# Second layer of a two-layer backbone: query latent and gates as seven products of quarters

## The chip, the cores and the metric

The kernel runs on one core of a Trainium2 chip. Its engines work side by side, each through its own list of instructions in order: TensorE (PE; its weight loads are listed apart as PEld), VectorE (DVE), ScalarE (ACT), GpSimd (POOL), and SyncE (SP), whose queue here issues nearly all DMAs; a few go through ScalarE's. TensorE writes to eight PSUM banks of 512 float32 per partition; everything else lies in SBUF (128 partitions) or in device memory. The metric is the device time of one execution in microseconds, the median over runs.

## The reference, cut to what matters

Two layers over 1024 latent tokens and 256 context tokens, width 1024. Layer 0 is windowed attention, layer 1 is multi-head latent attention, which is the last layer, so that context tokens need only keys and values there. For layer 1, with h the normed and modulated input:

```
cq, ckv, kr, g = split(h @ w_in, [512, 768, 800])      # 512 + 256 + 32 + 1024 columns
q  = rms_norm(cq, q_norm) @ w_uq                       # 16 heads x (64 + 32)
kv = rms_norm(ckv, kv_norm) @ w_ukv                    # 16 heads x (64 + 64)
qr, kr = rope(q[..., 64:]), rope(kr)
p  = softmax((qn . kn + qr . kr) * 96 ** -0.5)
y  = ((p @ v) * silu(g)) @ w_out
```

For the 1024 latent tokens, cq and g together are one product: 1536 channels, inner length 1024, 1024 tokens.

## The kernel before, in words

Every float32 operand of the large products is cut in two: a high half, rounded to the matmul's fp32r type by ScalarE, and a low half, the difference, mostly by VectorE or GpSimd (`split`, L272 and L273). `mm3` (L277 to L279) then makes three matmuls: high x high, low x high, high x low. So a product with 128 channels, inner length 1024 and 512 tokens is 8 x 3 = 24 matmuls of 512 columns.

Two large SBUF arenas, R (fp32r halves) and F (float32), are laid out by hand: `r_at` and `f_at` take an offset in KB per partition. PSUM banks are taken in turn (`pss`, `pst`).

The order of the instructions from late in layer 0's projections to the end of layer 1's projections isn't that of the program. A planner (`Plan`) records each operation with the operations that it must wait for (found by overlapping rectangles of memory, `rect`), and `emit` then lays them out by a simulation: each engine takes, of what is ready, the operation that comes first in the program; TensorE may reach 40 operations ahead. Durations and delays come from `Plan.cost` (for VectorE on 512 columns from SBUF 0.03 + 512 x 0.00106 us). What it lays out is each engine's fixed order; semaphores hold it to the dependencies at run time. After `plan.emit(tensor=5.0)` (L1834) the rest is issued in program order.

Layer 1 before the change goes through these stages:

- kv (L1437 to L1482): ten tiles of 128 tokens. Layer 0's result is loaded from `x1_d`, normed, turned by TensorE (`turn1`, L1368), scaled and shifted (`h1_part`), and cut into `hT1`: five buffers of 256 tokens, with input channels on the partitions. `kv_mm` makes 24 matmuls of 288 columns a tile. The latent's weights are loaded and cut meanwhile (`wq_cut`).
- query latent (`cq_tile`, L1262): eight tiles of 128 tokens, tokens on the partitions, 24 matmuls of 512 columns each (the first and last tile: 48 of 256). The squared sum of the row (L1206), its root, and a scaling by row and by `qn` follow; then four transposes (L1281) and a cut give `cqT` with channels on the partitions.
- queries (`qr_tile`, `qn_tile`): eight rotary tiles and sixteen others, 12 matmuls of 512 each; results are cut and stored to `qr_d` and `qn_d`. The rotary ones take a multiplication (L1300) and a shuffle (L1301) on VectorE and two operations on GpSimd (L1302, L1303).
- gates (`g_tile`, L1335): four blocks of 256 channels, each 2 x 2 tiles of 128 channels and 512 tokens, 24 matmuls, Silu on ScalarE (L1350), a store to `g1_d`. The last two blocks' tiles for the second token half (`gs`, L1835) aren't in the plan: they stand, in program order, between the first attention unit's top scores.
- attention, sixteen units of a head pair and 512 queries: `top` (L1623) makes high-half scores whose maxima VectorE reduces (L1629), `turn` (L1637) and `shift` (L1641) bring the maxima to the queries' side, `score` (L1657) makes the scores, ScalarE the exponentials, `PV` (L1680) the values' sum. A unit's top scores are made during the unit before it; the first unit has none before it.

```python
    gs = [g_tile(bi, 1, c, PB[:, 6 + c, :]) for bi in (8, 9) for c in range(2)]
    next(gs[0])
    for b in range(4):
        for i in range(3):
            units[0].top([(b, i)], (PB[:, 2 * i, :], PB[:, 2 * i + 1, :]))
        if b:
            next(gs[b])
        next(gs[b])
```

`make_V` (five pieces of 12 matmuls of 256 columns), `make_K` and `make_kr` prepare values and keys of the first heads.

Of the kernel before, what the change touches and what calls it, by code (L numbers as in the profile page):

```python
# [21 lines left out]
SEQ = 1024  # L22
# [45 lines left out]
class Plan:  # L68
# [9 lines left out]
    @staticmethod  # L78
    def rect(ap):
        t, dims = ap.tensor.name, [tuple(d) for d in ap.ap]  # L80
        row = int(np.prod(ap.tensor.shape[1:]))
        if t.split("_")[-1] == "d" or "_d_" in t or dims[0][0] != row:
            return t, 0, 1, ap.offset, ap.offset + sum(s * (n - 1) for s, n in dims) + 1
        p, f = divmod(ap.offset, row)
        return t, p, p + dims[0][1], f, f + sum(s * (n - 1) for s, n in dims[1:]) + 1
# [22 lines left out]
    def add(self, eng, name, fn, a, k, line):  # L108
# [7 lines left out]
        for w, xs in ((False, aps), (True, writes)):  # L116
            for x in xs:
                t, p0, p1, f0, f1 = self.rect(x)
# [91 lines left out]
def kernel(ctx: ExitStack, tc: tile.TileContext, t, out, dbg=None):  # L210
# [967 lines left out]
    wst1 = [96, 48, 96, 96, 48, 96, 48, 96, 48, 96]  # L1178
    ckvT = r_at(114, 2, 2, TOK)
    cqT = [r_at(64, 4, SEQ), r_at(134, 4, SEQ)]  # L1180
    cosb = f_at(0, 8, 32)
    sinb = f_at(1, 8, 32)
    qn = f_at(8, 512)
    kvn = f_at(66, 256)
    stg = Ring(F, [30, 32, 64.25], 512)
# [4 lines left out]
    ukV = r_at(64, 2, 2, 1024)  # L1190
# [3 lines left out]
    blocks1 = [("kv", 512, 288), ("cq", 0, 256), ("cq", 256, 256)]  # L1194
    blocks1 += [("qr", 1024, 512), ("qn", 0, 512), ("qn", 512, 512)]
    blocks1 += [("g", 800 + c * 256, 256) for c in range(4)]
    wt1 = {}

    def fetch1(bi, eng=None):
        kind, c0, n = blocks1[bi]  # L1200
        nk = 4 if kind[0] == "q" else 8
        wt1[bi] = r_at(wst1[bi], 2, nk, n)
        load_w(wt1[bi], t["b_w_uq"] if kind[0] == "q" else w_in1, stg, nk, n, lo_eng=eng, col0=c0)
# [15 lines left out]
    def kv_mm(ti):  # L1219
        p, j = ti // 2, ti % 2  # L1220
        W = wt1[0]
        kvps[ti] = ps = pss()
        for k in range(8):
            mm3(
                ps[:, 0:288],
                [hT1[p][:, s, k, j * 128 : j * 128 + 128] for s in range(2)],
                [W[:, s, k, :] for s in range(2)],
                k == 0, k == 7,
            )
# [29 lines left out]
    wcq = R[:, 48 * KB : 144 * KB].rearrange("p (c n) -> p c n", c=2)[:, :, 0 : 16 * KB]  # L1259
    wcq = wcq.rearrange("p c (s k n) -> p c s k n", s=2, k=8)  # L1260

    def cq_tile(ti):  # L1262
        p, j = (ti + 2) // 2, ti % 2
        ps = pss()
        for c in {0: (0, 1), 7: (1, 0)}.get(ti, (slice(0, 2),)):
            o = ps[:, c * 256 : c * 256 + 256] if ti in (0, 7) else shp(ps, 2, 256)
            for k in range(8):
                mm3(
                    o,
                    [hT1[p][:, s, k, j * 128 : j * 128 + 128] for s in range(2)],  # L1270
                    [wcq[:, c, s, k, :] for s in range(2)],
                    k == 0, k == 7,
                )
        r = rstd(ps, 512, sm_ring())
        e = ev.next()
        nc.vector.scalar_tensor_tensor(e, ps, r, qn, ALU.mult, ALU.mult)

        def rest():
            pt = shp(pst(), 4, 128)
            for c in range(4):  # L1280
                nc.tensor.transpose(pt[:, c, :], e[:, c * 128 : c * 128 + 128], ident)  # L1281
            ts = slice(ti * 128, ti * 128 + 128)
            split(cqT[0][:, :, ts], cqT[1][:, :, ts], pt)

        pend.append(rest)
# [3 lines left out]
    def qr_tile(c, half):  # L1289

        W = wt1[3]
        ts = slice(half * 512, half * 512 + 512)
        ps = pss()
        for k in range(4):
            mm3(
                ps, [W[:, s, k, c * 128 : c * 128 + 128] for s in range(2)], [cqT[s][:, k, ts] for s in range(2)],
                k == 0, k == 3,
            )
        a, r = ev.next(), ev.next()
        nc.vector.tensor_mul(a, ps, cosq[:, ts])  # L1300
        nc.vector.stream_shuffle(out=r, in_=ps, mask=swap1)  # L1301
        nc.gpsimd.tensor_mul(r, r, sinq[:, ts])  # L1302
        nc.gpsimd.tensor_add(a, a, r)  # L1303

        def rest():
            q = shp(qst.next(), 2, 512)
            split(q[:, 0].bitcast(F32R), q[:, 1].bitcast(F32R), a)
            load(out=qr_d[c, :, :, ts], in_=q)

        pend.append(rest)  # L1310

    def qn_tile(bi, pair, half):
        W = wt1[bi]
        c = pair % 4
        ts = slice(half * 512, half * 512 + 512)
        ps = pss()
        for k in range(4):
            mm3(
                ps, [W[:, s, k, c * 128 : c * 128 + 128] for s in range(2)], [cqT[s][:, k, ts] for s in range(2)],
                k == 0, k == 3,  # L1320
            )
        q = shp(qst.next(), 2, 512)
        split(q[:, 0].bitcast(F32R), q[:, 1].bitcast(F32R), ps)
        load(out=qn_d[pair, :, :, ts], in_=q)


    gpairs = [(2, 3), (4, 1)]
    gview = [
        R[:, o * KB : (o + 2 * d) * KB].rearrange("p (q n) -> p q n", q=2)[:, :, 0 : 16 * KB].rearrange(
            "p q (s k n) -> p q s k n", s=2, k=8  # L1330
        )
        for o, d in ((0, 16), (32, 48))
    ]

    def g_tile(bi, gp, c, ps=None):  # L1335

        c0 = blocks1[bi][1]
        W = wt1[bi]
        ps = pss() if ps is None else ps
        for k in range(8):  # L1340
            mm3(
                shp(ps, 2, 256),
                [W[:, s, k, c * 128 : c * 128 + 128] for s in range(2)],
                [gview[gp][:, :, s, k, :] for s in range(2)],
                k == 0, k == 7,
            )
            if k in (2, 5):
                yield
        gg = ev.next()
        nc.scalar.activation(gg, ps, AF.Silu)  # L1350
        ch = (c0 - 800) // 128 + c
        if gp == 0:
            load(out=g1_d[ch, :, 256:768], in_=gg)
        else:
            load(out=g1_d[ch, :, 768:1024], in_=gg[:, 0:256])
            load(out=g1_d[ch, :, 0:256], in_=gg[:, 256:512])
        yield

    def g_whole(bi, gp, c):
        for _ in g_tile(bi, gp, c):  # L1360
            pass
# [8 lines left out]
    def h1_part(p, b):  # L1370
        w = 1 if p == 0 else 0
        ps, h = tbank.pop((p, b)), shp(hr.next(), 2, 256)
# [3 lines left out]
        nc.vector.tensor_scalar(h[:, 0], ps[:, 0], sa[:, 0], sb[:, 0], ALU.mult, ALU.add)  # L1376

# [8 lines left out]
    wt1[0] = r_at(wst1[0], 2, 8, 288)  # L1386
# [6 lines left out]
    def w0_cut1(k, eng):  # L1393
        split(wt1[0][:, 0, k], wt1[0][:, 1, k], kws[k], eng)
# [50 lines left out]
    wq = {}  # L1445
    wq1 = Ring(F, [22, 24, 26, 28], 512)
    wq2 = Ring(F, [48, 50, 52, 54], 512)

    def wq_cut(c, i, eng):
        ks = slice(2 * i, 2 * i + 2)  # L1450
        split(wcq[:, c, 0, ks, :], wcq[:, c, 1, ks, :], wq[2 + 4 * c][i], eng)

    two = turn_two()
    for ti in range(NT):
# [15 lines left out]
        if ti in (2, 6):  # L1470
            wq[ti] = []
            for i in range(4):
                wq[ti].append(shp((wq1 if ti == 2 else wq2).next(), 2, 256))
                src = w_in1[i * 256 : i * 256 + 256, 64 * ti - 128 : 64 * ti + 128]
# [509 lines left out]
```

## Time and profile before

| what | value |
|---|---|
| median of 3 runs | 1500.04 us (1500.01 to 1501.14) |
| span of the profiled execution | 1499.7 us |
| profiled execution's own time | not listed apart; the runs' median is 0.3 us over the span |
| PE busy | 1479.0 us, 99% |
| DVE, POOL, ACT busy | 960.6, 850.2, 708.7 us |
| granted TensorE clock, mean | 0.997 |
| DMA, mean | 119 GB/s |
| kv stage, about | 682 to 720 us |
| query latent to first score | 720.35 to 940.72 us |

The page gives for each engine its busy time; the chain of waits follows the work that ended last back from the end. Matmuls are pipelined, so that the duration printed of one is longer than the distance between two starts; the distances say what a matmul costs. A row of the view in order of time has start, duration, engine, line, operation, tile written and read, shape, count, and in brackets how long the engine sat idle before and what ended that. A row of the view by groups has busy time and mean ns of one after the bar. A row of the view by stretches has the stretch, its length, and the busy us and instructions of PE, PEld, DVE, ACT and POOL, then granted clock, DMA share and GB/s.

### The profile page before, as it was taken

Reading aid. Unit: us, or ns where it says so; the run is one execution under the profiler, and the core shown is the slowest. Engines: PE = TensorE matmul, PEld = TensorE weight load, DVE = VectorE, ACT = ScalarE, POOL = GpSimd, SP = SyncE. Lnnn points to the kernel's source line nnn. Section 1 sums busy time; section 2 is a strip of 40 time slices with the busy share of each in tenths; the row PEclk is TensorE's granted clock in tenths of the full one; section 3 lists DMA queues with packets and bytes.
Section 4 is the critical chain, followed back from the end, with each engine's and each line's share of the span. In section 5 each row is a group of like instructions: output and inputs, shape, how many; then the busy total and the mean of one; then the engine's idle time right before and its main releaser. Section 6 shows DMA issues by size and latency. Waiting matters only on the chain.

```text
span 1499.7 us, 25035 instructions
## 1 busy us (share of the span) xinstructions
PE 1479.0 (99%) x9164; PEld 1203.9 (80%) x9164; DVE 960.6 (64%) x1869; ACT 708.7 (47%) x1363; POOL 850.2 (57%) x774
## 2 busy tenths in 40 slices
PE   6999999999999999999999999999999999999998
PEld 4888888888888888889888888776777767876687
DVE  4787788648778888878454004575566566566764
ACT  4421222369887888875233421453344434443322
POOL 2563365356454444457246510598788788789371
PEclk9999999999999999999999999999999999999999
DMA  9555644664354232334128622303121222121442
GB/s 338 164 170 170 209 157 166 212 209 117 120 159 126 86 108 89 95 120 135 35 85 287 198 70 85 92 15 79 47 60 54 62 63 60 47 59 34 154 155 85
DMA packets 128339, 178.93 MB, mean 119 GB/s; under 512 B 11980, under 2 KB 80716, under 8 KB 128216
## 3 DMA queue, kind: packets, MB, share of 16 engines
q1 hardware_dynamic: 123816, 170.67, 36.2%
q10 hardware_dynamic: 4400, 6.66, 1.3%
q8 instruction: 72, 1.18, 0.3%
q14 instruction: 51, 0.42, 0.1%
HBM read 131.13 MB, written 46.15 MB: 118 GB/s over the span
## 4 chain that ended last, share of the span: by engine, by line
PE 93%; DMA 2%; issue 2%; DVE 2%; POOL 1%; ACT 1%; SPq 0%; POOLq 0%; ACTq 0%; DVEq 0%
PE PB L277 15%; PE PB L278 15%; PE PB L279 15%; PE PB L1657 13%; PE PB L1680 9%; PE PB L729 5%; PE PB L1623 5%; PE PB L719 5%; PE PB L689 3%; PE PB L690 3%; PE PB L898 1%; PE PB L1691 1%; DMA arena_f<-x 1%; PE PB L748 1%; PE PB L903 1%
## 5 line engine op out<-in xcount | busy, mean ns | idle before, releaser
L277 PE MATMUL PB<-arena_r 128*128 128x512 f32 (+2 forms) x1240 | 452.0, 365 | 0.0
L278 PE MATMUL PB<-arena_r 128*128 128x512 f32 (+2 forms) x1240 | 446.0, 360 | 0.4 <-DVE arena_r L273 0.3
L279 PE MATMUL PB<-arena_r 128*128 128x512 f32 (+2 forms) x1240 | 445.5, 360 | 0.0
L1673 POOL TENSOR_TENSOR arena_f<-arena_f 128x1024 f32<-128x1024 f32 x120 | 285.7, 2381 | 8.2
L277 PEld LDWEIGHTS PB<-arena_r 128*128 128x128 f32 x1240 | 234.0, 189 | 44.4 <-issue 9.2
L279 PEld LDWEIGHTS PB<-arena_r 128*128 128x128 f32 x1240 | 233.9, 189 | 34.3
L278 PEld LDWEIGHTS PB<-arena_r 128*128 128x128 f32 x1240 | 234.1, 189 | 33.2 <-POOL arena_r L273 1.1
L1657 PE MATMUL PB<-arena_r 64*128 64x512 f32 (+1 forms) x1600 | 225.8, 394 | 0.0
L1629 DVE TENSOR_REDUCE krF<-PB 128x1 f32<-128x512 f32 (+1 forms) x264 | 167.3, 678 | 78.7 <-PE PB L1623 78.7
L1667 ACT ACTIVATE arena_f<-PB 128x1024 f32<-128x1024 f32 x160 | 164.2, 1026 | 111.6 <-PE PB L1657 83.6
L273 POOL TENSOR_TENSOR arena_r<-arena_f,arena_r 128x512 fp32r<-128x512 f32 (+1 forms) x98 | 132.6, 1368 | 143.0 <-ACT arena_r L272 128.7
L273 DVE TENSOR_TENSOR arena_r<-PB,arena_r 128x512 fp32r<-128x512 f32 (+2 forms) x215 | 139.9, 662 | 76.3 <-ACT arena_r L272 75.5
L1657 PEld LDWEIGHTS PB<-arena_r 64*128 64x128 f32 (+1 forms) x1600 | 176.5, 185 | 14.3 <-issue 5.2
L696 DVE CUSTOM_DVE_ANT_0 arena_f<-PB,arena_f,small 128x256 f32<-128x256 f32 (+1 forms) x288 | 148.3, 525 | 51.6 <-PE PB L690 33.3
L272 ACT CAST arena_r<-PB 128x512 fp32r<-128x512 f32 (+2 forms) x215 | 119.8, 563 | 110.1 <-PE PB L279 73.4
L1680 PE MATMUL PB<-arena_f 128*64 128x512 f32 x640 | 145.9, 595 | 0.0
L702 ACT ACTIVATE arena_f<-arena_f,small 128x640 f32<-128x640 f32 (+2 forms) x160 | 119.0, 744 | 15.5 <-DVE small L696 13.9
L499 DVE SCALAR_TENSOR_TENSOR arena_f<-arena_f,small 128x512 f32<-128x512 f32 x98 | 113.2, 1199 | 10.5 <-DMA arena_f<-ada_w 10.2
L729 PE MATMUL PB<-arena_r 128*128 128x512 f32 x336 | 118.6, 429 | 0.0
L1623 PE MATMUL PB<-arena_r 64*128 64x512 f32 (+1 forms) x768 | 109.4, 354 | 0.0
L719 PE MATMUL PB<-ident,arena_f 128*128 128x128 f32 x672 | 108.6, 272 | 0.1
L1680 PEld LDWEIGHTS PB<-arena_f 128*64 128x64 f32 x640 | 44.0, 137 | 79.6 <-issue 78.6
(189 smaller groups left out, 1972.6 us busy)
## 6 DMA issues: line engine op xcount, KB each, us to landing
arena_f<-ada_w SPq DMA_DIRECT2D x96, 256.0 KB, 3.9
arena_r<-q_d SPq DMA_DIRECT2D x160, 128.0 KB, 2.9
arena_f<-a_w_in SPq DMA_DIRECT2D x40, 256.0 KB, 3.8
arena_f<-x SPq DMA_DIRECT2D x16, 512.0 KB, 6.1
q_d<-arena_f SPq DMA_DIRECT2D x16, 512.0 KB, 3.0
qn_d<-arena_f SPq DMA_DIRECT2D x16, 512.0 KB, 4.7
arena_r<-qn_d SPq DMA_DIRECT2D x16, 512.0 KB, 5.3
arena_f<-b_w_in SPq DMA_DIRECT2D x24, 256.0 KB, 4.5
```

The lines of the kernel that those rows point to most:

```text
L273: (lo_eng or nc.vector).tensor_sub(lo, src, hi.bitcast(F32))
L277: nc.tensor.matmul(o, ah, bh, start=first, stop=False)
L278: nc.tensor.matmul(o, al, bh, start=False, stop=False)
L279: nc.tensor.matmul(o, ah, bl, start=False, stop=last)
L719: nc.tensor.transpose(pt[:, h, :], self.Ps[h][:, ci * 128 : ci * 128 + 128], ident)
L729: nc.tensor.matmul(self.pv, V[:, self.chunks[ci], self.g, :], PT[:, s], start=ci == 0 and s == 0, stop=ci == self.m - 1 and s == 1,)
L1623: nc.tensor.matmul(bank[:, o : o + n], self.q[r, s, bs], k[r, 0, n0 : n0 + n], start=s == 0, stop=s == 2)
L1629: nc.vector.reduce_max(self.mxp[:, e, b : b + 1, i], bank[:, 0:n], AX.X)
L1657: nc.tensor.matmul(PB[:, b + e, :], k[r, s, cs], q[r, sq], start=i == 0, stop=i == 4)
L1667: nc.scalar.activation(E, PB[:, b : b + 2, :], AF.Exp)
L1673: eng.tensor_add(acc, acc, E)
L1680: nc.tensor.matmul(PB[r, 7, :], Vq[:, c, h, :], E[:, e], start=c == 0, stop=c == NT - 1)
```

## The change

Query latent and gates become one product of weights (as rows: 1536 channels) with activations, in six sets of 256 channels: two of the latent, four of gates. In each set the weights A (256 channels x 1024) and the activations B (1024 x 1024 tokens) are cut into quarters, and Winograd's form of Strassen's scheme gives the four quarters of the result by seven products of quarters, where the plain way has eight. A product is 128 channels, inner length 512, 512 tokens: `product`, 4 x 3 = 12 matmuls.

- The activations' four combinations (`t_make`, T1 to T4) are made once, for all sets, in float32 by VectorE, and cut (`t_cut`). For that, `h1_part` also copies each scaled tile from SBUF to SBUF by DMA into `hF` (sixteen copies of 256 KB on SP's queue). T1 and T4 overwrite quarters of `hT1` that are done with.
- The weights' four combinations (`s_make`) are made per set, on VectorE, a set ahead. Weights come in quarters of 128 channels by 512 rows, 256 KB each (`w_load`), 36 loads, two quarters of a set twice.
- First come the six products A11 B11 (kept in SBUF by ScalarE), then the six A12 B21, whose sum is a result quarter, then per set the other five (`set_steps`), whose sums are put together by VectorE from PSUM. Sets go in the order 0, 2, 1, 3, 4, 5, where 0 and 1 are the latent's.
- The query latent comes out with channels on the partitions, so its 32 transposes fall away. The row scale is now found by summing squares over sets and partitions (`cq_sums`, eight matmuls of one column), spread over the partitions by GpSimd and eight transposes (`cq_spread`), and applied to the queries: in the rotary tables, and by a multiplication of each other query tile. `q_norm` goes into the query weights as they are cut (`q_cut`).
- All queries now come behind the gates. The last eight query tiles are in the plan with `make_kr` and `make_K`; `make_V`, in five pieces, takes the place of the gate tiles between the first unit's top scores.
- The planner's rectangles are finer: an access with up to four widely spaced parts counts as several rectangles, and bf16 offsets are put in words.

The code that the diff adds or moves, cut:

```diff
+    def product(W, B):
         ps = pss()
         for k in range(4):
+            m = [B(s, k) for s in range(2)]
+            mm3(ps if len(m[0].shape) == 2 else shp(ps, 2, 256), [W[s][:, k] for s in range(2)], m, k == 0, k == 3)
+        return ps
...
+    def done(i, c, t, x):
+        if i > 1:
+            nc.scalar.activation(x, x, AF.Silu)
+            tok_store(g1_d[2 * i - 4 + c], x, t)
+            return
+        dst = cqT[2 * i + c, t]
+        split(dst[:, 0], dst[:, 1], x)
+        sq = x if summed[t] else acc[t]
+        nc.scalar.activation(sq, x, AF.Square)
+        if summed[t]:
+            nc.vector.tensor_add(acc[t], acc[t], x)
+        summed[t] += 1
+
+    def t_make(k):
+        f1, f2, f3, f4 = (shp(f[:, k], 2, 256) for f in (F1, F2, F3, F4))
+        nc.vector.tensor_sub(f1, H12(k), H11(k))
+        nc.vector.tensor_sub(f2, H22(k), f1)
+        nc.vector.tensor_sub(f3, H22(k), H12(k))
+        nc.vector.tensor_sub(f4, H21(k), f2)
...
+    def s_make(st):
+        a11, a21, a22, a12, s1 = st
+        nc.vector.tensor_add(s1, a21, a22)
+        nc.vector.tensor_sub(a21, a11, a21)
+        nc.vector.tensor_sub(a11, s1, a11)
+        nc.vector.tensor_sub(a12, a12, a11)
+        for x in (a11, a21, s1, a12, a22):
+            yield w_cut(x)
+
+    def set_steps(i, W):
+        p1 = p1s[i]
+        ps = product(W[0], T2)
+        q = outs.next()
+        nc.vector.tensor_add(q, ps, p1)
+        yield
+        p7 = product(W[1], T3)
+        yield
+        ps = product(W[2], T1)
+        r, x = outs.next(), outs.next()
+        nc.vector.tensor_add(r, ps, q)
+        nc.vector.tensor_add(x, p7, r)
+        nc.vector.tensor_add(q, p7, q)
+        done(i, 1, 1, x)
+        yield
+        ps = product(W[3], B22)
+        nc.vector.tensor_add(r, ps, r)
+        done(i, 0, 1, r)
+        yield
+        ps = product(W[4], T4)
+        nc.vector.tensor_add(q, ps, q)
+        done(i, 1, 0, q)
+        yield
...
+    def qn_tile(bi, c, t):
+        ps = q_mm(bi, c, t)
+        e = ev.next()
+        nc.vector.tensor_mul(e, ps, rbc[t])
+        q_out(qn_d[4 * bi - 4 + c], e, t)
...
+        if p:
+            load(out=hF[p][:, 2 * b : 2 * b + 2, :], in_=h)
...
+    for i, o in enumerate((8, 10, 6, 12, 2, 4)):
+        ps = product(W1[i], B11)
+        p1s[i] = f_at(o, 512)
+        nc.scalar.copy(p1s[i], ps)
+        flush()
+        if i == 0:
+            W1[5] = w_cut(a11[5])
+            a12[5] = w_load(a11r.next(), 5, 0, 1)
+        if i < 4:
+            t_cut(T2, F2, i)
+            t_cut(T1, F1, i)
+        for j in {3: (2, 3), 4: (4, 5), 5: (0, 1)}.get(i, ()):
+            a12r[j] = w_cut(a12[j])
+    W = []
+    ops = iter(())
+    for n, i in enumerate((2, 3, 4, 5, 0, 1)):
+        ps = product(a12r[i], B21)
+        x = outs.next()
+        nc.vector.tensor_add(x, ps, p1s[i])
+        done(i, 0, 0, x)
+        if n == 1:
+            ops = s_make(st.pop())
+            st.append(s_load(1, order[1]))
+        if n:
+            W += [w for _, w in zip(range(1), ops)]
+        if n < 4:
+            t_cut(T3, F3, n)
+            t_cut(T4, F4, n)
...
     plan.emit(tensor=5.0)
-    gs = [g_tile(bi, 1, c, PB[:, 6 + c, :]) for bi in (8, 9) for c in range(2)]
-    next(gs[0])
+    fillb = Banks(6, 7)
+    vk = make_V(0)
+    next(vk)
     for b in range(4):
         for i in range(3):
             units[0].top([(b, i)], (PB[:, 2 * i, :], PB[:, 2 * i + 1, :]))
-        if b:
-            next(gs[b])
-        next(gs[b])
+        next(vk)
```

368 lines of the change are left out of this document (200 added, 168 removed).

## The prediction

> **What bounds the kernel now.** I read the page's busy shares and its chain of waits first, to see which engine sets the end.
>
> ```profile
> span 1499.7 us, 25035 instructions
> PE 1479.0 (99%) x9164; PEld 1203.9 (80%) x9164; DVE 960.6 (64%) x1869; ACT 708.7 (47%) x1363; POOL 850.2 (57%) x774
> PE 93%; DMA 2%; issue 2%; DVE 2%; POOL 1%; ACT 1%; SPq 0%; POOLq 0%; ACTq 0%; DVEq 0%
> ```
>
> TensorE (PE) is busy 99% and carries 93% of the chain, so a matmul removed is worth its pitch, provided the other engines keep up. The average says nothing of the stage that changes, so the second view is the instructions in order of time: it gives the ends of the stage and the pitch of its matmuls.
>
> ```profile
> 720.35 0.36 PE L277 MATMUL PB<-arena_r 128*128 128x256 f32 x1
> ...
> 723.07 0.28 PE L278 MATMUL PB<-arena_r 128*128 128x256 f32 x1
> ...
> 724.51 0.28 PE L278 MATMUL PB<-arena_r 128*128 128x256 f32 x1
> ...
> 728.50 0.39 PE L277 MATMUL PB<-arena_r 128*128 128x512 f32 x1
> ...
> 730.54 0.39 PE L277 MATMUL PB<-arena_r 128*128 128x512 f32 x1
> ...
> 737.62 1.03 PE L1281 MATMUL PB<-ident,arena_f 128*128 128x128 f32 x8
> 738.41 0.48 PE L277 MATMUL PB<-arena_r 128*128 128x512 f32 x1
> ...
> 938.76 0.44 PE L1637 MATMUL PB<-ident,krF 128*64 128x128 f32 x4
> 939.13 0.50 PE L277 MATMUL PB<-arena_r 128*128 128x512 f32 x1
> ...
> 940.72 0.97 PE L1657 MATMUL PB<-arena_r 64*128 64x512 f32 x6
> ```
>
> The printed 0.39 us is a latency; starts give the pitch. From 728.50 to 730.54 there are nine 512-wide matmuls: 0.227 us each. From 723.07 to 724.51 there are twelve of 256: 0.120 us. Eight transposes take 0.79 us (737.62 to 738.41): 0.10 each. The stage begins with the first query-latent matmul at 720.35 and ends with the first score matmul at 940.72: 220.4 us. The third view is busy time by stretch:
>
> ```profile
> core 0: us, PE busy (x) PEld busy (x) DVE busy (x) ACT busy (x) POOL busy (x), PEclk, DMA share, GB/s
> 720.30:940.70 220.40, 220.12 (x1091) 183.37 (x1089) 68.87 (x121) 62.38 (x118) 76.13 (x64) 1.00 0.38 125
> 682.00:727.00 45.00, 44.07 (x347) 43.74 (x346) 37.56 (x94) 23.16 (x62) 31.86 (x40) 1.00 0.28 88
> 660.00:682.00 22.00, 22.00 (x126) 18.95 (x125) 15.90 (x27) 17.00 (x39) 12.28 (x14) 1.00 0.77 252
> ```
>
> PE fills the stretch, VectorE (DVE) uses 68.9 of 220.4 us, and the clock is full. Matmuls bound this stage; DVE has room, and the change spends that room.
>
> **The change, part by part.** *Matmuls.* Before, query latent and gates cost 6 tiles x 24 of 512, 2 tiles x 48 of 256, and 16 gate tiles x 24 of 512: 528 x 0.227 + 96 x 0.120 = 131.4 us. After, six sets of seven products of 12 matmuls, 504 x 0.227 = 114.4 us: **-17.0 us**. The 24 query tiles, the twelve matmuls each, keys and values stay.
>
> *Transposes.* 32 of the latent go; 8 that spread the row scale come: 24 x 0.10 = **-2.4**. Eight one-column matmuls for the sums of squares are new; the nearest row is the four small matmuls L1637, 0.37 us from 938.76 to 939.13, so about 0.09 each: **+0.7**. With nothing hidden worse than before, that is -18.7.
>
> *Work moved to DVE and ScalarE.* I need the price of a DVE operation with both inputs in SBUF, with GpSimd (POOL) idle and not.
>
> ```profile
> L603 DVE TENSOR_TENSOR arena_r<-arena_f,arena_r x8: 684/685/686, 258.4 to 276.1; 64x512 fp32r<-64x512 f32 x8
> L273 DVE TENSOR_TENSOR arena_f<-PB,arena_f 128x512 fp32r<-128x512 f32 x16 | 11.0, 689 | 24.3 <-ACT arena_f L272 24.3
> 783.50 1.11 DVE L273 TENSOR_TENSOR arena_f<-arena_f 128x512 fp32r<-128x512 f32 x1
> L1302 POOL TENSOR_TENSOR arena_f<-arena_f 128x512 f32<-128x512 f32 x8 | 10.4, 1296 | 1.5 <-DVE arena_f L1301 1.5
> L1301 DVE STREAM_SHUFFLE arena_f<-PB 128x512 f32<-128x512 f32 x8 | 6.0, 747 | 0.0
> L499 DVE SCALAR_TENSOR_TENSOR arena_f<-arena_f,small x98: 730/752/1857, 72.8 to 297.4; 128x512 f32<-128x512 f32 x98
> L272 ACT CAST arena_r<-arena_f 128x512 fp32r<-128x512 f32 x44 | 26.3, 623 | 21.6 <-DMA arena_f<-b_w_ukv 7.9 <-DMA arena_f<-b_w_in 6.0 <-DMA arena_f<-b_w_uq 5.0
> 738.45 0.58 ACT L272 CAST arena_r<-PB 128x512 fp32r<-128x512 f32 x1
> 739.06 0.69 DVE L273 TENSOR_TENSOR arena_r<-PB,arena_r 128x512 fp32r<-128x512 f32 x1 [0.32 <-ACT arena_r L272]
> ```
>
> 0.69 us from either memory; 1.11 us where POOL's rotary multiply runs beside it. Counted from the code, DVE has in the product stage: 16 differences of the activations; 62 low halves (16 for the four combinations T, 8 first factors left over, 30 for the combined weights, 8 for the latent); 24 combinations of weights; 42 additions of products; 6 sums of squares. 150 x 0.69 = 103 us beside 114.4 us of matmuls. The cover holds, but 90% full where it was 31%. ScalarE has 62 casts at 0.62, 6 copies at 0.58 and 24 functions at about 0.6, some 56 us: covered. It is tightest at the start: the first six products need only ready factors, but the second six need more cuts, and the third row T2 after twelve products, 12 x 12 x 0.227 = 32.7 us. By then DVE owes some 16 differences, 24 cuts, 6 additions and the first set's 9: 55 x 0.69 = 38 us, of which a third of the differences can run in the idle DVE time of the stage before (45.0 - 37.6 = 7.4 us). 38 - 5 = 33 against 32.7, and an order laid out by the planner at 0.573 us per operation (its cost line), 17% too short. So a stall from 0 to 38 - 32.7 = 5.3 us; nearer the low end, since T1, T3 and T4 are wanted one to four products later: **+2**. Six PSUM banks let PE run five products ahead of the additions after that.
>
> *Stage before: copies of the activations.* Sixteen 256 KB SBUF copies are added on SP's queue; each waits for the scaled tile, and behind it stand layer-input and weight loads. Four of them fall into the crowded stretch (660 to 682, 252 GB/s), where 1 MB takes 4 us; the later ones meet DMA at 28%. The inputs so delayed are due several tiles later, and PE's slack was 0.9 us. Between 0 and 4, nearer the low end for that lead: **+1**.
>
> *Query tiles.* DVE: rotary tiles 8 x (0.69 + 0.75 + 1.11), others 16 x 1.38, twelve scaled cuts at 0.75, eight value and key cuts at 0.69, 57 us under 24 x 12 x 0.227 = 65 us. The first scaled cuts fall into the last set, where no weights are made. No cost; if cover fails, the banks lend 13 us first. Stores become 36 issues on SP instead of 24, at under 0.5 us each, also covered.
>
> *The first unit's maxima.* Here a cover is removed. Four gate tiles stood between the groups of top-score matmuls; five pieces of V stand there now.
>
> ```profile
> 914.00 1.43 PE L1623 MATMUL PB<-arena_r 64*128 64x512 f32 x12
> 919.00 1.43 PE L1623 MATMUL PB<-arena_r 64*128 64x512 f32 x12
> L1629 DVE TENSOR_REDUCE krF<-PB 128x1 f32<-128x512 f32 x20 | 12.5, 684 | 13.3 <-PE PB L1623 13.3
> L1629 DVE TENSOR_REDUCE krF<-PB 128x1 f32<-128x256 f32 x8 | 3.0, 415 | 0.0
> L1634 DVE TENSOR_REDUCE krF<-krF 128x8 f32<-128x24 f32 x1 | 0.2, 178 | 0.0
> 939.25 1.41 DVE L1641 TENSOR_TENSOR arena_r<-PB,ident 4x512 fp32r<-4x512 f32 x2 [2.04 <-PE PB L1637]
> 941.52 0.62 PE L1623 MATMUL PB<-arena_r 64*128 64x512 f32 x4
> ```
>
> Reductions: 16 x 0.684 + 8 x 0.415 = 14.3 us, 3.6 a group; PE has 1.43 + 12 x 0.120 = 2.9 a group. DVE now sets the pace. From the end of the last query product: 1.44 of V, 0.5 for the first tops, about 0.3 of hand-over, 14.3 of reductions, 0.2, 0.4 turn, 1.4 shift, 0.3: 18.9 us. PE's own work there is 4 x 1.43 + 5 x 1.44 + 0.4, and the part of the first score that does not need the shift (0.97 + 0.62): 14.9. Hole 4.0; with two hand-overs more, **+4.5**. The bounds are 0 (the reductions hide as before) and 6.0 (18.9 less 12.9 of tops and V, none of the score ahead).
>
> *Sum*, against the profiled execution's 1499.7 us of span and the 0.3 us by which the median of the runs, 1500.04, exceeds it: 1500.0 - 18.7 + 2 + 1 + 4.5 = 1488.8, say **1489 us**.
>
> **The rivals.** *No cover is missed* (1481.5): matmul count alone. For it: PE lost 0.3 us in 220 before. Against: 3.6 us of reductions cannot hide behind 2.9.
>
> *DVE and ScalarE in turn become the bound of the products* (1495.5): each of the 62 cuts waits for a cast, 0.32 us in the row above; if DVE, which takes its work in order, idles so each time, 103 + 62 x 0.32 = 123 us, 8.5 beyond 114.4, in place of the 2. For it: the planner's short price. Against: casts are cheap (0.58) and can run ahead.
>
> *The clock drops at the first unit.*
>
> ```profile
> 28.00:32.00 4.00, 3.19 (x25) 2.71 (x25) 2.23 (x7) 3.09 (x6) 0.78 (x2) 1.00 1.05 388
> 1490.00:1499.00 9.00, 3.94 (x33) 3.74 (x32) 3.01 (x9) 1.93 (x7) 0.55 (x1) 0.88 0.15 58
> ```
>
> PE busy 80% kept clock 1.00; busy 44% it fell to 0.88. There PE will be busy about 14.9 of 19 us, 78%. If 0.88 held for the 18 us after, 18 x (1/0.88 - 1) = 2.5 us: 1491.5. The Trainium skill, "TensorE: Matmul & The Clock Gate", section "HAM oscillation — how this bites in real kernels", warns that idle gaps of more than about 3.4 us put the array at half rate; an estimate by that page is 1.7 us lost in one such window, and the pieces here are under 1 us apart from the shift, so by it too the drop is unlikely.
>
> *Slower: DVE against POOL.* If the product stage's DVE work takes 1.11 us as at 783.50, 150 x 1.11 = 167 us replaces 114.4: 1489 - 2 + 52 = 1539. It overtakes matmuls from 114.4/150 = 0.76 us, and eats the whole gain from about 0.85 us. Against: POOL gets only copies and one power in that stage; the rotary multiplies come after.
>
> *Weights late* (1506): 36 loads of 256 KB with rows of half the length replace 24; if in-order issue behind result stores cost each of six sets 3 us, +18. Against: DMA stood at 0.38 over the stretch, and a set's loads go out a set (13.6 us) ahead.
>
> **How the numbers follow.** Forecast 0.52, DVE bound 0.22, nothing missed 0.12, clock 0.05, POOL 0.05, weights 0.04. The range 1481.5 to 1497 takes in the first four, some 0.85 after their own spread. A measurement of this kernel tells about 0.2% (3 us) from no change: slower 0.08 (the last two, less their mild forms), same 0.05 (the bad tail of DVE bound), faster 0.87.
>
> **What would show it.** Right: 504 matmuls of 512 in the product stage at pitch 0.227; DVE 85 to 90% there; some 17 us from the last query product to the first score, with PE waiting for the maxima's reductions. Wrong: PE idle more than 5 us between first and last product, waiting for DVE (bound) or for weights (DMA); DVE means near 1.1; the kv stage longer by more than 4 us; granted clock under 1.

## The result, and the profile after

The kernel after takes **1492.84 us** (median of four runs, 1492.38 to 1493.13) against 1500.59 us (median of four, 1500.01 to 1501.17) for the kernel before: ratio 0.9947, 95% interval 0.9932 to 0.9961. That is 7.75 us, or 0.5%, faster. The prediction was 1489 us, with a range from 1481.5 to 1497.

The profiled execution has a span of 1491.1 us, where the one before had 1499.7: 8.6 us less. First the page's busy shares and chain of waits of the kernel after:

```profile
PE 1462.2 (98%) x9036; PEld 1185.1 (79%) x9036; DVE 1062.6 (71%) x2029; ACT 734.4 (49%) x1397; POOL 810.8 (54%) x735
PE 90%; DVE 4%; DMA 2%; issue 2%; POOL 1%; ACT 1%; SPq 0%; POOLq 0%; DVEq 0%; ACTq 0%
```

PE is busy 16.8 us less, and its share of the chain fell from 93% to 90%; DVE's rose from 2% to 4%. There are new places where the matmuls wait for DVE: from 660 to 745 us PE waited once, 0.9 us, before the change, and seven times, 5.7 us, after it (experiment 1 shows the rows of after). The view of before (what PE wrote, whom it waited for, us in total, times, longest), and the first transposes of the key/value stage before and after:

```profile
PE PB L1368 <- DVE arena_f L1376: 0.9, 1, 0.9
...
665.97 1.91 PE L1368 MATMUL PB<-ident,arena_f 128*128 128x128 f32 x16
...
666.75 1.91 PE L1454 MATMUL PB<-ident,arena_f 128*128 128x128 f32 x16
```

The view by stretches (columns as in the prediction: stretch, length, busy time and instructions of PE, PEld, DVE, ACT, POOL, then granted clock, DMA share, GB/s) finds them:

```profile
682.00:727.00 45.00, 41.94 (x312) 40.02 (x310) 41.31 (x97) 26.72 (x68) 32.01 (x35) 1.00 0.52 170
724.00:731.00 7.00, 4.37 (x20) 3.05 (x20) 7.00 (x22) 5.88 (x14) 2.74 (x4) 1.00 0.13 31
731.00:845.00 114.00, 114.00 (x516) 94.67 (x517) 93.69 (x149) 55.49 (x94) 3.26 (x3) 1.00 0.46 129
913.00:932.00 19.00, 17.85 (x136) 15.03 (x137) 16.25 (x32) 5.66 (x9) 0.00 (x0) 1.00 0.84 242
```

From 731 to 845 us, nearly all of the products, PE never stands still, and DVE is busy 82%. The cost lies at the two ends. In the key/value stage PE has 41.94 of 45 us (before: 44.07), in the seven microseconds at the start of the products 4.37, with DVE at 7.00 of 7.00, and behind the last query product 17.85 of 19. In order of time, PE's instructions there:

```profile
724.06 0.44 PE L1249 MATMUL PB<-ident,arena_f 128*128 128x128 f32 x2 [0.95 <-DVE arena_f L1236]
724.25 0.48 PE L285 MATMUL PB<-arena_r 128*128 128x512 f32 x1
727.51 0.44 PE L1249 MATMUL PB<-ident,arena_f 128*128 128x128 f32 x2 [0.26 <-DVE arena_f L1236]
730.96 0.44 PE L1249 MATMUL PB<-ident,arena_f 128*128 128x128 f32 x2 [2.31 <-DVE arena_f L1236]
...
914.86 0.28 PE L285 MATMUL PB<-arena_r 128*128 128x256 f32 x1
...
929.79 0.44 PE L1767 MATMUL PB<-ident,krF 128*64 128x128 f32 x4 [1.15 <-DVE krF L1764]
930.16 0.97 PE L1787 MATMUL PB<-arena_r 64*128 64x512 f32 x6
```

L1249 turns the last key/value tiles. These transposes stand in PE's order ahead of the first product, behind it, and inside the second one. They wait for L1236, the row scaling on DVE, which comes late. What DVE does meanwhile:

```profile
725.78 0.68 DVE L1328 TENSOR_TENSOR arena_f<-arena_r,arena_f 128x512 f32<-128x512 f32 x1
726.38 0.68 DVE L1329 TENSOR_TENSOR arena_f<-arena_r 128x512 f32<-128x512 f32 x1
726.98 0.48 DVE L1236 SCALAR_TENSOR_TENSOR arena_f<-PB,small,arena_f 128x256 f32<-128x256 f32 x1
...
728.24 0.68 DVE L281 TENSOR_TENSOR arena_r<-arena_f,arena_r 128x512 fp32r<-128x512 f32 x1
728.84 0.14 DVE L1204 TENSOR_SCALAR small<-small 128x1 f32<-128x1 f32 x1
728.90 0.68 DVE L1330 TENSOR_TENSOR arena_f<-arena_r,arena_f 128x512 f32<-128x512 f32 x1
729.50 0.41 DVE L281 TENSOR_TENSOR arena_r<-PB,arena_r 128x256 fp32r<-128x256 f32 x1
729.83 0.68 DVE L281 TENSOR_TENSOR arena_r<-arena_f,arena_r 128x512 fp32r<-128x512 f32 x1
730.43 0.47 DVE L1236 SCALAR_TENSOR_TENSOR arena_f<-PB,small,arena_f 128x256 f32<-128x256 f32 x1
...
917.22 12.31 DVE L1759 TENSOR_REDUCE krF<-PB 128x1 f32<-128x512 f32 x24
```

The activations' differences (L1327 to L1330) and the cuts (L281) stand between the pieces of the key/value tiles. Such a tile's chain goes back and forth between engines: a squared sum on ScalarE, the small L1204 on DVE, a power on GpSimd (L1205), then L1236 on DVE. In the rows, L1204 starts at 728.84 and L1236 at 730.43, and DVE has no idle time between. The prediction had looked for the stall at the thirteenth product, the first that uses T2; it sits at the first and second, at transposes that the change doesn't touch.

The account in profiled time: key/value stage from its first transposes to the first product 54.4 us before (665.97 to 720.35) and 57.5 after (666.75 to 724.25), **+3.1**; first product to first score 220.4 and 205.9, **-14.5**; first score to the end of the span 559.0 and 560.9, **+1.9**, of which 1.4 lies between the issue of the last output's DMA and the end; and the key/value stage began 0.8 us later, in a part that the change doesn't reach. The sum is -8.7 us, and the spans differ by -8.6.

### The profile page after: what moved, and what is told of

Read it like the earlier page. It is cut to its first block, busy times and chain, and to the rows that moved or that the text cites. A ratio compares the mean times of both kernels' runs of the same rounds, so it can differ in the third digit from the quotient of the medians.

```text
span 1491.1 us, 25085 instructions
## 1 busy us (share of the span) xinstructions
PE 1462.2 (98%) x9036; PEld 1185.1 (79%) x9036; DVE 1062.6 (71%) x2029; ACT 734.4 (49%) x1397; POOL 810.8 (54%) x735
## 4 chain that ended last, share of the span: by engine, by line
PE 90%; DVE 4%; DMA 2%; issue 2%; POOL 1%; ACT 1%; SPq 0%; POOLq 0%; DVEq 0%; ACTq 0%
PE PB L285 15%; PE PB L286 14%; PE PB L287 14%; PE PB L1787 13%; PE PB L1810 9%; PE PB L737 5%; PE PB L727 5%; PE PB L1753 5%; PE PB L697 3%; PE PB L698 3%; PE PB L1821 1%; PE PB L906 1%; DVE krF L1759 1%; PE PB L756 1%; PE PB L911 1%
## 5 line engine op out<-in xcount | busy, mean ns | idle before, releaser
L285 PE MATMUL PB<-arena_r 128*128 128x512 f32 (+2 forms) x1200 | 439.3, 366 | 0.0
L286 PE MATMUL PB<-arena_r 128*128 128x512 f32 (+2 forms) x1200 | 433.7, 361 | 0.0
L287 PE MATMUL PB<-arena_r 128*128 128x512 f32 (+2 forms) x1200 | 433.3, 361 | 0.0
L285 PEld LDWEIGHTS PB<-arena_r 128*128 128x128 f32 x1200 | 226.3, 189 | 44.3 <-issue 9.0
L287 PEld LDWEIGHTS PB<-arena_r 128*128 128x128 f32 x1200 | 226.3, 189 | 33.6
L286 PEld LDWEIGHTS PB<-arena_r 128*128 128x128 f32 x1200 | 226.4, 189 | 32.1 <-POOL arena_r L281 0.6
L1787 PE MATMUL PB<-arena_r 64*128 64x512 f32 (+1 forms) x1600 | 228.1, 395 | 0.0
L280 ACT CAST arena_r<-PB 128x512 fp32r<-128x512 f32 (+2 forms) x207 | 115.3, 563 | 113.8 <-PE PB L287 73.3
L281 DVE TENSOR_TENSOR arena_r<-PB,arena_r 128x512 fp32r<-128x512 f32 (+2 forms) x207 | 134.3, 661 | 34.8 <-ACT arena_r L280 34.2
L281 POOL TENSOR_TENSOR arena_r<-arena_f,arena_r 128x512 fp32r<-128x512 f32 (+1 forms) x64 | 87.8, 1386 | 103.1 <-ACT arena_r L280 86.9
L280 ACT CAST arena_r<-arena_f 128x512 fp32r<-128x512 f32 (+1 forms) x142 | 82.6, 610 | 83.1 <-PE PB L287 33.0
L1753 PE MATMUL PB<-arena_r 64*128 64x512 f32 (+1 forms) x768 | 111.5, 354 | 0.0
```

Of the source, the lines that this page charges most:

```text
L280: nc.scalar.copy(hi, src)
L281: (lo_eng or nc.vector).tensor_sub(lo, src, hi.bitcast(F32))
L285: nc.tensor.matmul(o, ah, bh, start=first, stop=False)
L286: nc.tensor.matmul(o, al, bh, start=False, stop=False)
L287: nc.tensor.matmul(o, ah, bl, start=False, stop=last)
L1753: nc.tensor.matmul(bank[:, o : o + n], self.q[r, s, bs], k[r, 0, n0 : n0 + n], start=s == 0, stop=s == 2)
```

## The experiments

Twelve runs of eleven kernels (experiment 1 was timed twice), in three groups, each group timed against the kernel before on one chip. The medians of before were 1501.02, 1500.58 and 1501.01 us. All start from the kernel after.

**1. Late turns.** The last key/value tiles' transposes are written out behind the third product instead of behind the first.

```diff
-        flush()
+        if i > 1:
+            flush()
```

> The last two key/value tiles' transposes stand behind the third product instead of behind the first; nothing else is changed. Theory: in the changed kernel PE waits 4.0 us for VectorE in front of these transposes (rows L1249), because the differences of the activations fill VectorE's list there, while the products behind them could run. Then these waits go, and the time falls from 1492.8 by 2.5 to 4 us, to about 1489.5 (0.9925 of the kernel before). Rival: VectorE is behind with everything, and the wait only moves to the first product that needs a late cut: no change, 1492.8.

Measured 1487.43 us (1486.84 to 1488.66), ratio 0.9912 [0.9897, 0.9927]; a second time, as the base of the third group, 1487.41 us (1487.28 to 1487.93), 0.9908 [0.9895, 0.9922]. PE's waits from 660 to 745 us, in after and then in late turns:

```profile
PE PB L1249 <- DVE arena_f L1236: 4.0, 4, 2.3
PE PB L1454 <- ACT arena_f L1461: 1.1, 2, 0.6
PE PB L1454 <- DVE arena_f L1462: 0.6, 1, 0.6
```

```profile
PE PB L1249 <- DVE arena_f L1236: 1.4, 2, 0.9
...
```

The wait in the first products is gone, and no product waited instead: the stall came from the place of these transposes in PE's order. That it was the activations' differences and the cuts that made L1236 late is read from DVE's list, where DVE is busy 7.00 of 7 us; no run here shows it by itself. This version beats both kernels, by 5.4 us against after. By the rows the edit itself is worth about 2.6 us of waits (0.26 + 2.31) and their restarts; of the other 2 to 3 us, 1.1 and 1.5 lie ahead of the key/value stage and some 0.9 at the last output in the two profiled executions, where the instructions are the same. In the opening the granted clock is low in all three, but later in after: 0.92, 0.50 and 0.90 in the five-us stretches from 15 us, against 0.58, 0.73, 1.00 and 0.72, 0.60, 1.00 in the two of late turns. PE is busy about 2 of 5 us in the first of these stretches and over 4 in the other two, so a later fall meets more matmuls; that this makes the 1.1 and 1.5 us is likely and not shown. What makes the end differ stays open.

> The kernel with the late turns once more, as the base for the three beside it on this chip: 1486.5 to 1488.5 us. If its gain is TensorE's 2.9 us of waiting plus a drop of the granted clock that follows that wait in some executions, every execution here has a mean clock of 0.997 or more and none has a stretch below full clock between 30 and 1480 us.

The profiled execution of the second time shows the clock below 1.00 only up to 25 us and in the last 5 us. The mean clock says less than expected: this execution had 0.996, since the mean counts the stretches at both ends. A fall of the clock behind the stall (last section) isn't the rest of the gain either: the profiled execution of after had none from 30 to 1480 us, and took 1492.88 us.

**2. The eighth product.** One of the seven products of each set is made twice into the same bank, where the second time writes over the first: 72 matmuls more.

```diff
-        for k in range(4):
+        for k in [*range(4)] * times:
...
-        p7 = product(W[1], T3)
+        p7 = product(W[1], T3, 2)
```

> In each of the six sets one product is made twice into the same bank (the second writes over the first): 72 more matmuls of 512, eight products' worth of TensorE work a set, all else as in the changed kernel. Theory (matmuls set the pace of the product stage): 72 x 0.227 = 16.3 us more, 1492.8 + 16.3 = 1509, slower than the kernel before. Rival (VectorE sets the pace of that stage): the matmuls go into TensorE's waits, less than 5 us more, below 1498.

Measured 1508.02 us, ratio 1.0048 [1.0033, 1.0063]: 15.2 us above after, 0.21 us for each matmul, where the pitch is 0.227. The page:

```profile
PE 1478.2 (98%) x9108; PEld 1203.3 (80%) x9108; DVE 1062.8 (71%) x2029; ACT 734.2 (49%) x1397; POOL 810.5 (54%) x735
```

With DVE's work unchanged, PE's busy time and the span grow by 16.0 and 14.5 us. Matmuls still bound the products; with eight products to a set the kernel after would have been slower than the one before.

**3 and 4. DVE's room.** In one kernel DVE makes the low halves of the combined weights twice (30 operations more); in another GpSimd makes them instead.

```diff
-            yield w_cut(x)
+            cut = w_cut(x)
+            nc.vector.tensor_sub(cut[1], shp(x, 4, 128), cut[0].bitcast(F32))
+            yield cut
```

```diff
-            yield w_cut(x)
+            yield w_cut(x, nc.gpsimd)
```

> The low half of each combined weight in the sets is computed twice, 30 more VectorE operations of about 0.6 us, 18 us more on VectorE, none on TensorE. VectorE is busy 93.7 of 114 us in the product stage, so it would be full (112 of 114). Theory (matmuls set the pace, VectorE has room): at most 3 us more, 1493 to 1496. Rival (VectorE in turn with ScalarE sets the pace): most of the 18 us shows, 1505 or more.

> The 30 low halves of the combined weights are made by GpSimd instead of VectorE, the situation of the prediction's slower rival: a GpSimd operation with two SBUF inputs runs beside VectorE's. GpSimd has 30 x 1.3 = 39 us of work there, VectorE 18 us less of its own, and each of its operations between two SBUF operands may take 1.1 us instead of 0.69. Theory: VectorE's loss stays under its relief of 18 us, and the weights are made a set ahead, so no change, 1492 to 1495. Rival: operations at 1.1 us put VectorE past the matmuls: 1500 or more.

Measured 1493.58 us (0.9951 [0.9934, 0.9968]) and 1492.24 us (0.9939 [0.9925, 0.9954]): both as after, within the noise. The stretch of the products in the first and the one new wait there, and then, by groups, DVE's and GpSimd's cuts from 724 to 850 us in the second:

```profile
731.00:845.00 114.00, 111.64 (x497) 92.39 (x498) 108.19 (x175) 52.03 (x88) 3.26 (x3) 0.99 0.43 119
```

```profile
808.63 1.27 PE L1387 MATMUL PB<-small,arena_f 128*128 128x1 f32 x8 [1.53 <-DVE arena_f L1322]
```

```profile
L281 POOL TENSOR_TENSOR arena_r<-arena_f,arena_r 128x512 fp32r<-128x512 f32 x30 | 43.2, 1446 | 59.0 <-ACT arena_r L280 46.1 <-PE PB L286 6.8 <-DVE arena_f L1361 4.7
L281 DVE TENSOR_TENSOR arena_r<-arena_f,arena_r 128x512 fp32r<-128x512 f32 x36 | 28.4, 825 | 3.6 <-ACT arena_r L280 3.4
```

DVE at 108 of 114 us still does not bound; one wait of 1.5 us appears, at the sums of squares, and in this execution the clock fell behind it (0.76 from 806 to 813 us; see the last section). With GpSimd beside it a DVE cut takes 0.825 us on average, in place of 0.689 in after, and that costs nothing either. In after itself DVE stands idle 2.8 us in all ahead of its 66 cuts in that stretch, and GpSimd is busy 3.26 of 114 us. So neither "DVE and ScalarE in turn" nor "DVE against POOL" is this kernel.

**5. No copies.** The sixteen copies between SBUF buffers are left out; the differences use the high halves alone.

```diff
-        (lambda k, t=t, k0=k0: hview[t][:, :, k0 + k]) for t, k0 in ((0, 0), (0, 4), (1, 0), (1, 4))
+        (lambda k, t=t, k0=k0: gview[t][:, :, 0, k0 + k].bitcast(F32)) for t, k0 in ((0, 0), (0, 4), (1, 0), (1, 4))
...
-        if p:
-            load(out=hF[p][:, 2 * b : 2 * b + 2, :], in_=h)
```

> The sixteen SBUF copies of the scaled activations are left out; the differences of activations are formed from the high halves alone, so the low halves' part is missing in the four combinations T. Everything else stays. Theory (the 3.1 us that the key/value stage is longer come from VectorE's list, where first-factor cuts and differences stand ahead of the pieces that the key/value tiles wait for): no more than 1 us is gained, 1492 to 1493 us. Rival (copies on SP's queue delay the loads of layer inputs, the prediction's term of +1, bounds 0 to 4): 1489 to 1490.5 us, and the gaps of 0.6 to 1.1 us in the key/value stage go away.

Measured 1491.99 us (1490.26 to 1492.72), 0.9941 [0.9927, 0.9954]. PE's waits from 660 to 745 us:

```profile
PE PB L1249 <- DVE arena_f L1236: 3.5, 2, 2.1
PE PB L1454 <- ACT arena_f L1461: 0.9, 1, 0.9
PE PB L1454 <- DVE arena_f L1462: 0.8, 2, 0.6
```

5.2 us of waits where after has 5.7. DMA is busy 0.30 from 682 to 725 us where after has 0.55, and PE waits nearly as before. From its first transposes to the first score this execution takes 264.4 us, after 263.4. A fall of the granted clock (0.72 from 728 to 734 us; see the last section) adds about 1.6 us here, an estimate; less that, the execution without copies is 0.6 us shorter. The medians differ by 0.85 us. So the copies cost about 1 us at most, and the prediction's term for them gave the wrong reason for a loss that is there.

**6. Early top scores.** Nine of the twelve groups of the first unit are moved between the last eight query tiles. For that, the keys' preparation comes before these tiles, and their products take four PSUM banks in turn instead of six.

```diff
+            for _ in range(2 if i in (3, 6) else 1):
+                j = 9 - len(tops0)
+                units[0].top([tops0.pop(0)], tbanks[j % 2])
...
-        for i in range(3):
+        for i in range(3 if b == 3 else 0):
```

> Nine of the first unit's twelve top-score groups are moved between the last eight query tiles, so that their reductions lie beside query products; three groups stay behind the last query product. Theory (TensorE stands still 2.0 us between last query product and first score, because reductions of 12.3 us set the pace there): 1.5 to 2.5 us are gained, 1490.5 to 1491.3 us, and the stretch from last query product to first score is shorter by as much beside the groups moved. Rival (VectorE is as full under the query tiles, so the reductions only move the wait there): 1492.5 to 1493.5 us.

Measured **1496.16 us** (1493.87 to 1497.79), 0.9966 [0.9955, 0.9976]: 3.3 us slower than after. Both the theory and the rival fell. In order of time:

```profile
910.74 0.39 PE L287 MATMUL PB<-arena_r 128*128 128x512 f32 x1
911.06 0.73 PE L1753 MATMUL PB<-arena_r 64*128 64x512 f32 x4
...
912.06 0.39 PE L286 MATMUL PB<-arena_r 128*128 128x512 f32 x1
...
914.35 0.39 PE L287 MATMUL PB<-arena_r 128*128 128x512 f32 x1
914.67 0.50 PE L1753 MATMUL PB<-arena_r 64*128 64x256 f32 x4
...
915.44 0.40 PE L286 MATMUL PB<-arena_r 128*128 128x512 f32 x1
...
923.34 0.38 PE L285 MATMUL PB<-arena_r 128*128 128x256 f32 x1 [0.68 <-DVE krF L1759]
...
933.47 0.44 PE L1767 MATMUL PB<-ident,krF 128*64 128x128 f32 x4 [1.13 <-DVE krF L1764]
```

From 910.74 to 912.06 lie two query matmuls, 0.227 each, and four top matmuls of 512 columns: these take 1.32 - 0.45 = 0.87 us. From 914.35 to 915.44 it is the same with 256 columns: 0.64 us. So 256 columns on four matmuls are worth 0.23 us. If the other 256 are worth as much, 0.64 - 0.23 = 0.4 us are left that no column pays for. **Going from 128-row to 64-row matmuls and back costs about 0.4 us of PE here**, and the idle column shows nothing of it. Eight such changes there and back in place of four make 1.6 us; the wait for the last maxima stays, 1.13 us, since the last three groups still come last, and one of 0.68 is new. In the profiled execution the clock also fell at the start of the products (0.73 from 729 to 735 us), which cost about 1.6 us. From first product to first score it takes 209.9 us, after 205.9; the three losses, 1.6 + 1.6 + 0.7, make up 3.9 of these 4.0 us.

**7 and 8. Late cuts, and all together.** The cuts of four first factors are moved two key/value tiles later, and one more tile's turns behind a product, on top of late turns; then the same with the early top scores.

```diff
-        if 4 <= ti < 8:
-            i = ti - 4
+        if 6 <= ti < 10:
+            i = ti - 6
...
-        flush(1)
+        if ti < NT - 1:
+            flush(1)
```

> As the kernel with the late turns (1487.4 us), and the cuts of four first factors stand at key/value tiles 6 to 9 instead of 4 to 7, and the turns of one more key/value tile come behind a product. Theory (VectorE's list is too full in the key/value stage, and whatever TensorE waits for there, 0.6 to 1.1 us at a time, stands behind cuts that are not yet wanted): 1 to 2.5 us below the kernel with the late turns, 1485 to 1486.5 us. Rival (these small gaps come from the evacuations of the turned tiles themselves, whatever else is in the list): 1487 to 1488 us, or later, since the cuts then come too late for the first products.

> Late turns, late first-factor cuts and early top scores together. If the three waits are separate and each is filled: the sum of the gains, 1483.5 to 1485.5 us. If the product and query stages then run VectorE full, or one wait only moves to the next place: 1486.5 us or more.

Measured 1492.65 us (0.9948 [0.9935, 0.996]) and 1495.35 us (0.9966 [0.9953, 0.9978]): 5.2 and 7.9 us above late turns alone. The late cuts' rows:

```profile
728.19 7.31 DVE L281 TENSOR_TENSOR arena_r<-arena_f,arena_r 128x512 fp32r<-128x512 f32 x12
735.41 0.42 DVE L281 TENSOR_TENSOR arena_r<-PB,arena_r 128x256 fp32r<-128x256 f32 x1
...
735.89 0.69 PE L1249 MATMUL PB<-ident,arena_f 128*128 128x128 f32 x2 [4.36 <-DVE arena_r L281]
...
736.80 0.63 PE L286 MATMUL PB<-arena_r 128*128 128x512 f32 x1
737.23 0.63 PE L287 MATMUL PB<-arena_r 128*128 128x512 f32 x1
```

and the stretch behind the wait:

```profile
736.00:741.00 5.00, 5.00 (x14) 4.00 (x15) 4.96 (x10) 2.00 (x4) 0.00 (x0) 0.56 0.48 123
```

Twelve cuts now stand in a row on DVE, and the one that empties the turned tiles' PSUM bank comes behind them, at 735.41. So PE waits 4.36 us for a bank. Then the matmuls go at 0.43 us each in place of 0.227, until 740.2. The work moved off one wait became a longer one. With the early top scores too the same wait is 4.35 us.

**9. The last piece.** On top of late turns, the first of V's five pieces goes from ahead of the first top scores to behind the last of them.

```diff
     vk = make_V(0)
-    next(vk)
...
         next(vk)
         if b == 3:
+            next(vk)
```

> As the late turns, and the first of the five pieces of V stands no longer ahead of the first unit's top scores but behind the last of them, as a second piece there. The matmuls stay the same, the first reduction starts 1.4 us earlier. Theory (the hole of 1.3 us there is the reductions' pace from a late start): the hole goes, 1.0 to 1.5 us below the late turns. Rival (the top scores then wait for their banks, one group behind the other): same as the late turns, with waits ahead of the second to fourth group in place of the hole.

Measured 1487.54 us (1487.12 to 1489.05), 0.991 [0.9897, 0.9924]: as late turns. The rival held:

```profile
910.72 1.43 PE L1754 MATMUL PB<-arena_r 64*128 64x512 f32 x12
913.71 2.85 PE L1754 MATMUL PB<-arena_r 64*128 64x512 f32 x12
...
```

No wait is left ahead of the turn of the maxima, but the second group takes 2.85 us, where the others take 1.43 to 1.50: its weight loads wait three times for L1760, 1.0 us in all, since the reductions give the banks back at their own pace. From the last 512-wide query matmul to the first score pass 15.6 us, in late turns 15.5. So the hole comes from the length of the reductions, wherever PE meets it.

**10 and 11. First factors' low halves on GpSimd**, with late turns; then with the last piece too.

```diff
-            W1[i] = w_cut(a11[i])
+            W1[i] = w_cut(a11[i], nc.gpsimd)
```

> As the late turns, and the low halves of the four first factors that are cut in the key/value stage are made by GpSimd, so that VectorE's list there is shorter by eight operations. Theory (TensorE's waits of 0.6 to 1.1 us in that stage come from these cuts in VectorE's list): most of the 4.3 us of gaps between 683 and 724 us goes, 1.5 to 3 us below the late turns. Rival (the waits are the turned tiles' own evacuations with two banks, whoever makes the cuts): within 0.7 us of the late turns.

> Late turns, the last piece of V and the cuts on GpSimd together: the sum of the two gains if they are separate, 1483 to 1485.5 us; if the cuts on GpSimd bring nothing, 1486 us.

Measured 1488.88 us (1486.94 to 1489.74; 0.9914 [0.9901, 0.9928]) and 1487.36 us (1486.54 to 1490.47; 0.9911 [0.9898, 0.9925]): nothing gained. The waits of experiment 10 from 660 to 745 us:

```profile
PE PB L1249 <- DVE arena_f L1236: 2.5, 1, 2.5
...
```

Three small waits went and one of 2.5 us came: with 1.2 us at L1454 that is 3.7 us, where late turns has 2.4 to 3.3. Ahead of the late L1236 stand an activations' difference on DVE, 1.75 us long there, and the power on GpSimd. Behind this wait the clock fell too (0.66 from 716 to 721 us), which takes about 1.6 us more from this execution, an estimate. So it isn't the cuts by themselves.

## Why the prediction was right or wrong

**Matmuls, transposes, sums of squares (-18.7): right as far as it was tested.** From the first product to the first score 14.5 us went, and the waits there, 2.6 us in the first products and about 2 at the maxima, make up the difference to within half a microsecond. Between 731 and 845 us there is no idle time of PE, and the eighth product put back 15.2 us of the 16.3 that its 72 matmuls are worth at 0.227.

**DVE in the products (covered): right, at a price that was too high.** The rows print 0.68 us, but starts without idle time are 0.60 apart (725.78, 726.38, 726.98). 150 x 0.60 = 90 us, which is nearer to the 93.7 busy in 114 (82%) than the 103 forecast (90%). The planner's 0.573, which the prediction called 17% short, is 5% short of that.

**Stall at the start (+2): the size near, the place wrong.** It was put at T2, whose cuts were never waited for. PE waited 0.26 + 2.31 us at the key/value tiles' transposes, behind the same full DVE list. Experiment 1 shows the place. That the size came near is luck: the sum for it counted the work due by the thirteenth product.

**Key/value stage (+1, bounds 0 to 4): mis-sized, with the wrong reason.** It measured 3.1 us, of which 2.2 are waits of PE (3.1 us of them in the stage, before 0.9). The copies on SP's queue were blamed; without them 0.5 us of waits goes. DVE went from 37.6 to 41.3 of 45 us in that stage, which the prediction used as free time (7.4 us) and did not price as a delay to the stage's own chain. Which of the operations there is to blame is not settled: with the cuts moved later or to GpSimd, another stands in front.

**First unit's maxima (+4.5): mis-sized.** From 914.86 to 930.16 pass 15.3 us, where the prediction had some 17; PE's own work there is 14.9 less the score's 1.6, so the hole is about 2: 1.15 us of wait, and the rest without idle time, as in the changes of rows of experiment 6. The reductions were priced by their printed durations, 14.3 us; in a row they take 12.31.

**The base, and luck.** Every run's time is about 1.8 us over its own span (1492.88 to 1491.1), not 0.3. So the profiled execution of before took about 1501.5 us, an estimate, which is above the runs listed for it. The stages that the change touches moved by -14.5 + 3.1 = -11.4 us, where the forecast had -11.2 (1500.0 to 1488.8). That these agree is luck, for the errors of the terms cancelled: 2.6 + 3.1 + 2 for 2 + 1 + 4.5. The spans differ by less, 8.6 us, because 0.8 us were lost in the opening and 1.9 behind the first score. The second recurs in the other kernels here (559.4 to 561.2 us from first score to the end, before 559.0), and its cause wasn't found. So the miss from 1488.8 to 1492.8 lies mostly outside the sum: 1.5 (base) + 0.8 + 1.9 - 0.2 = 4.0 us.

**The rivals.** "The clock drops" had the mechanism and not the place: nothing dropped at the first unit, where PE is busy 17.85 of 19 us at clock 1.00, but the clock fell elsewhere in some executions, as the last section shows. "DVE and ScalarE in turn" and "DVE against POOL" fell by experiments 3 and 4, "Weights late" by the full stretch of products.

## What to carry to other kernels

When work moves to an engine with room, its average doesn't say who pays. A short chain that passes through that engine many times, and whose end has a fixed place in the matmuls' order, can come late behind the long operations put between its pieces. Here it was best to move the waiting matmuls later first (one line; no other version is faster than it beyond the noise). Moving the other operations instead, to a later place (experiment 7) or to GpSimd (experiment 10), only moved the wait. And a run of operations is better priced by the distance of its starts than by the printed duration.

## What the runs showed of the hardware

**The clock fell to half behind waits of 1.5 us and more, in some executions.** The stall of 2.31 us again, in the execution with the weights' low halves on GpSimd, and its stretches:

```profile
728.99 0.69 PE L1249 MATMUL PB<-ident,arena_f 128*128 128x128 f32 x2 [2.31 <-DVE arena_f L1236]
...
730.33 0.63 PE L287 MATMUL PB<-arena_r 128*128 128x512 f32 x1
730.76 0.63 PE L285 MATMUL PB<-arena_r 128*128 128x512 f32 x1
```

```profile
722.00:729.00 7.00, 4.35 (x20) 3.02 (x20) 7.00 (x22) 5.91 (x14) 2.74 (x4) 0.94 0.11 25
729.00:735.00 6.00, 6.00 (x15) 4.77 (x16) 6.00 (x12) 2.51 (x5) 0.00 (x0) 0.50 0.24 58
```

The granted clock is 0.50 for 6 us, and the pitch 0.43 us. In the profile of after the same wait, 2.31 us at 730.96, was followed by 1.00 (the stretch from 731 quoted above). PE had been busy 4.35 of 7 us in the one and 4.37 in the other. So a stall can cost its length and, in some executions, about 13 matmuls at 0.2 us more, 2.6 us.

Of the thirteen traces of the changed kernel and its variants, seven have such a fall between 680 and 820 us, each behind a wait of 1.5 to 4.4 us (experiments 3 to 8 and 10). Waits of 2.3 to 2.5 us left the clock at 1.00 in after, in experiments 2 and 11, and at 731 us in experiment 3. The three traces with no wait above 1 us there (late turns twice, experiment 9) have no fall. What decides between the two, the runs don't show. The Trainium skill, "TensorE: Matmul & The Clock Gate", section "HAM oscillation — how this bites in real kernels", gives idle gaps of more than about 3.4 us as what throttles the array to half. The half rate agrees with 0.50; the gap here was shorter, 2.31 us behind several small ones, and the measurement decides.

**Going from 128-row to 64-row matmuls and back cost about 0.4 us** (experiment 6), which no idle time shows. **Reductions from PSUM** follow each other faster than they print: 24 in 12.31 us, 0.51 each, where the prediction's rows print 0.684 (512 columns) and 0.415 (256).
